# The last MLP of a two-layer trunk, its first products in pairs with seven block products in place of eight

## The chip, the cores and the metric

The kernel runs on one core of a Trainium2 chip. The metric is the device time of one execution in microseconds (us), the median of several runs. A profile of one more execution gives the times of every instruction.

## What is computed

A sequence of 528 positions (16 learned ones ahead of 512 real ones) with 1024 features goes through two layers, each a mixer followed by a squared-ReLU MLP, all float32. What the change touches is the MLP of the last layer; the learned positions are dropped at the end, so it works on 512 positions:

```python
def _sq_relu_mlp(hn, w1, w2):
    a = jax.nn.relu(hn @ w1)
    return (a * a) @ w2
...
h = h + _sq_relu_mlp(_rmsnorm(h, norm_mlp[layer]), mlp_w1[layer], mlp_w2[layer])
h = _rmsnorm(h, norm_final)
return h[:, N_META:, :]
```

Here `w1` is 1024x4096 and `w2` 4096x1024. `_rmsnorm` divides each position by the root of the mean of its squares and multiplies by a gain per feature.

## The kernel before

Activations lie feature-major: a tile has 128 features on the partitions and the positions along the free dimension. The weights come from memory as 225 units of 128x1024 (512 KB); a unit is eight 128x128 blocks, as a rule one block of 128 output features against 1024 inputs. Float32 accuracy is had from three products of a reduced format: every operand is split into a high part (a cast, ScalarE, lines 120 and 169) and a low part (the difference, VectorE, line 117), and each block costs three matmuls: high·high, high·low, low·high.

`emit_load` (line 149) brings a unit into `raw` (two buffers) and splits it into `wh` and `wl` (three buffers each). For the units in the set `POOL_L`, which holds 161 and 164 of the last MLP, GpSimd makes the low part. `get_w` keeps the loads two units ahead of use. `unit_mm` (line 206) multiplies a unit with eight pairs of activation tiles: in the last MLP 24 matmuls of 512 columns into one PSUM bank out of the four of `mmp`.

`mlp` (line 681) is used for both layers. `norm_x` (line 255) multiplies each of the eight tiles of `h` with the gain and splits it; the squares are summed on GpSimd (`nsq`, line 273). The reciprocal root (`norm_r`, line 276: four matmuls with a matrix of ones, then ScalarE and VectorE) is not applied to the input but to the output of the first product. It is asked for after the first unit. There are four quarters `q`, and each has eight first units, whose output goes through line 692 (VectorE: max with 0, times the root), line 694 (ScalarE: square), a cast (line 120) and a difference (line 117) into the activation tiles `a0` to `a7`, and then eight second units, whose output VectorE adds to `h` (line 705). The second units of the last quarter, units 217 to 224, are kept in eight buffers of their own, and `final_quarter` (line 958) uses them the other way round (positions on the partitions, lines 973 to 997), followed by the last norm and the stores. The chain of the last MLP alone is thus units 161 to 216 and then those eight.

In the first MLP (line 708) `make_ahead` (line 185) runs after every second unit: it brings the 32 units 129 to 160 into SBUF by DMAs from GpSimd's queue, splits them and writes both parts back to memory, from where the attention layer reads them without a split.

The order of instructions on each engine is made by a list scheduler at compile time: an instruction's priority is its place in the program, and `soon()` moves it ahead by 568 places. Each engine then runs its list in that order and waits at each instruction for what it needs.

Of the kernel before, what the change touches and what calls it, by code (L numbers as in the profile page):

```python
# [10 lines left out]
F32 = mybir.dt.float32  # L11
F32R = mybir.dt.float32r
# [4 lines left out]
P = 128  # L17
# [4 lines left out]
KB = 8  # L22
# [33 lines left out]
POOL_L = {5, 33, 43, 44, 52, 126, 161, 164}  # L56
N_S = 31

AHEAD = range(129, 161)

# [22 lines left out]
def trunk(tc, hT, wu, wri, pk, lv, rope, gf, out, probe=None):  # L83
# [7 lines left out]
    with ctx:  # L91
# [14 lines left out]
        def sc(name, dt=F32, w=T):  # L106

            return big.tile([P, T], dt, tag="s", name=name, bufs=N_S)

        def xt(name):  # L110
# [13 lines left out]
        pkt = cp.tile([P, N_PK], F32, name="pkt")  # L124
        nc.sync.dma_start(out=pkt, in_=pk)
        ones = cp.tile([P, P], F32, name="ones")
# [10 lines left out]
        def soon():  # L137
            return tc.high_priority(offset=BOOST)
# [11 lines left out]

        def emit_load():
            i = state["next"]
            u = seq[i]
            if i in AHEAD:
                wh, wl = (wp.tile([P, 1024], F32R, tag="w" + p, name=f"w{p}{i}") for p in "hl")
                for w, part in zip((wh, wl), parts[i - AHEAD[0]]):
                    nc.sync.dma_start(out=w.bitcast(F32), in_=part)
                ready.append((wh, wl))
                state["next"] += 1
                return  # L160
            raw = wr.tile([P, 1024], F32, tag="raw", name=f"raw{i}")
            nc.sync.dma_start(out=raw, in_=wu[u])
            if u >= N_UNIT - 8:
                wh, wl = (wp.tile([P, 1024], F32R, tag="wf" + p, name=f"w{p}{i}", bufs=8) for p in "hl")
            else:
                wh = wp.tile([P, 1024], F32R, tag="wh", name=f"wh{i}")
                wl = None if u == U_GATE else wp.tile([P, 1024], F32R, tag="wl", name=f"wl{i}")
            with soon():
# [30 lines left out]

        def get_w(u):  # L200
            while state["next"] <= min(state["use"] + 2, len(seq) - 1):
                emit_load()
            assert seq[state["use"]] == u
            state["use"] += 1
            return ready.pop(0)
# [107 lines left out]
        ident = cp.tile([P, P], F32, name="ident")  # L313
        make_identity(nc, ident)
        onesr = cp.tile([P, P], F32R, name="onesr")
# [249 lines left out]
        def conv_in(b):  # L565
            i, pr = b % 2, b // 2
            if ("gw", pr) not in lru:
                rawg = wr.tile([P, 512], F32, tag="rawg", name="rawg", bufs=1)
# [112 lines left out]
        def mlp(u0, gc, lo, tag, last=None, between=None):  # L681
            n = T - lo
            mx, terms = norm_x(h, gc, lo, tag)
            for q in range(4):
                a = []
                for j in range(KB):
                    ps = unit_mm(u0 + q * 16 + j, mx, lo, n)
                    if q == j == 0:
                        rs, _ = norm_r(terms, lo, tag)
                    t = sc("rt")  # L690
                    for p, tk in ps:
                        nc.vector.scalar_tensor_tensor(out=t[:, tk], in0=p, scalar=0.0, in1=rs[:, tk],  # L692
                                                       op0=ALU.max, op1=ALU.mult)
                    nc.scalar.activation(out=t[:, lo:], in_=t[:, lo:], func=AF.Square)  # L694
                    a.append(xt(f"a{j}"))
                    split(a[j], t[:, lo:], slice(lo, T))
                    if between and j % 2:
                        between()
                if q == 3 and last:
                    last(a)  # L700
                else:
                    for c in range(KB):
                        ps = unit_mm(u0 + q * 16 + 8 + c, a, lo, n)
                        for p, tk in ps:
                            nc.vector.tensor_tensor(out=h[:, c, tk], in0=p, in1=h[:, c, tk], op=ALU.add)  # L705
                        if between and c % 2:
                            between()

        mlp(U_MLP0, C_NMLP0, 0, "m", between=make_ahead)
# [26 lines left out]
        mkf = cp.tile([P, P], F32, name="mkf")  # L736
# [3 lines left out]
        mkr = cp.tile([P, P], F32R, name="mkr")  # L740
        nc.vector.tensor_copy(out=mkr, in_=mkf)
        idr = cp.tile([P, P], F32R, name="idr")
# [10 lines left out]
        for pair in kz:  # L753
            for c in range(2):
                nc.gpsimd.memset(pair[c][64 - 64 * c:128 - 64 * c, :].bitcast(F32), 0.0)
# [56 lines left out]
        def attn_steps(hd, rot, vr):  # L812
# [54 lines left out]
            def tstep(I):  # L867
                if I == 0:
                    st["pp"] = big.tile([P, 2, 1792], F32R, tag="y", name="pp")
# [74 lines left out]
        gfr = big.tile([P, 1024], F32, tag="gf", name="gfr")  # L944
        nc.sync.dma_start(out=gfr, in_=gf.partition_broadcast(P))
        h_t = []

        def turn_h(t):

            r = big.tile([P, 1024], F32, tag="ht", name="ht", bufs=4)  # L950
# [47 lines left out]
        mlp(U_MLP1, C_NMLP1, NM, "n", last=final_quarter)  # L998


def lay_out(x, meta_tokens, norm_mix, norm_mlp, norm_final, ab_w_in, ab_if_bias, mlstm_norm, lru_conv_w, lru_conv_b,
# [8 lines left out]
    def put(u, m):  # L1010
        wu[u, :, :, :m.shape[1]] = m.reshape(KB, P, m.shape[1]).transpose(1, 0, 2)
# [16 lines left out]
    for l, u0 in ((0, U_MLP0), (1, U_MLP1)):  # L1028
        for q in range(4):
            for j in range(8):  # L1030
                s = q * 1024 + j * P
                put(u0 + q * 16 + j, mlp_w1[l][:, s:s + P])
                if u0 + q * 16 + 8 == N_UNIT - 8:
                    wu[N_UNIT - 8 + j] = mlp_w2[l][s:s + P, :].reshape(P, KB, P)
                    continue
                put(u0 + q * 16 + 8 + j, mlp_w2[l][q * 1024:(q + 1) * 1024, j * P:(j + 1) * P])
# [57 lines left out]
```

## Time and profile before

| | us |
|---|---|
| three runs | 1461.93, 1464.75, 1466.83 (median 1464.75) |
| the profiled execution, its own time | 1463.24 |
| span of its instructions | 1461.4 |
| TensorE busy | 1437.9 |
| VectorE busy | 814.5 |
| ScalarE busy | 650.8 |
| GpSimd busy | 214.0 |

The span is what the profile sees, from the first to the last instruction; 1.84 us of the execution lie around it. The mean granted clock of TensorE is 0.999 of full speed. Busy time of TensorE counts an instruction from its start to its modelled end, so neighbouring matmuls overlap in it, and what a stage costs is better read from the distance of their starts.

### The profile page before, as it was taken

Reading aid. Unit: us, or ns where it says so; the run is one execution under the profiler, and the core shown is the slowest. Engines: PE = TensorE matmul, PEld = TensorE weight load, DVE = VectorE, ACT = ScalarE, POOL = GpSimd, SP = SyncE. Lnnn points to the kernel's source line nnn. Section 1 sums busy time; section 2 is a strip of 40 time slices with the busy share of each in tenths; the row PEclk is TensorE's granted clock in tenths of the full one; section 3 lists DMA queues with packets and bytes.
Section 4 is the critical chain, followed back from the end, with each engine's and each line's share of the span. In section 5 each row is a group of like instructions: output and inputs, shape, how many; then the busy total and the mean of one; then the engine's idle time right before and its main releaser. Section 6 shows DMA issues by size and latency. Waiting matters only on the chain. (4 is left out here: it accounts for less than half of the span.)

```text
span 1461.4 us, 24650 instructions
## 1 busy us (share of the span) xinstructions
PE 1437.9 (98%) x9970; PEld 1338.6 (92%) x9970; DVE 814.5 (56%) x1423; ACT 650.8 (45%) x1154; POOL 214.0 (15%) x286
## 2 busy tenths in 40 slices
PE   8999999999999999999999999999999999999998
PEld 8999999999999999999999998989887888888886
DVE  6867754667544545545445568777755344343452
ACT  6454743647334424334334536565644223142342
POOL 4000001010012231322314511101031000000001
PEclk9999999999999999999999999999999999999999
DMA  7332224231223685857857875555332332333331
GB/s 255 98 116 80 89 72 133 60 101 59 88 87 102 217 272 175 266 183 234 283 180 245 297 230 156 170 158 181 124 116 88 100 91 97 98 90 101 89 126 46
DMA packets 70046, 210.11 MB, mean 144 GB/s; under 512 B 13066, under 2 KB 14615, under 8 KB 69932
## 3 DMA queue, kind: packets, MB, share of 16 engines
q1 hardware_dynamic: 53996, 157.15, 34.4%
q0 software_dynamic: 15360, 50.34, 10.4%
q8 instruction: 78, 1.28, 0.4%
q10 hardware_dynamic: 576, 1.05, 0.2%
q14 instruction: 36, 0.29, 0.1%
HBM read 162.11 MB, written 35.71 MB: 135 GB/s over the span
## 5 line engine op out<-in xcount | busy, mean ns | idle before, releaser
L169 ACT CAST wh<-raw 128x1024 fp32r<-128x1024 f32 x193 | 202.6, 1050 | 503.7 <-PE mm L220 402.8
L117 DVE TENSOR_TENSOR wl<-raw,wh 128x1024 fp32r<-128x1024 f32 x184 | 227.1, 1235 | 66.9 <-ACT wh L169 66.5
L705 DVE TENSOR_TENSOR h<-mm,h 128x264 f32<-128x264 f32 (+1 forms) x88 | 41.2, 498 | 109.8 <-PE mm L220 109.8
L117 DVE TENSOR_TENSOR ral<-ra,rah 128x512 fp32r<-128x512 f32 x64 | 43.7, 688 | 56.4 <-ACT rah L120 56.4
L120 ACT CAST rah<-ra 128x512 fp32r<-128x512 f32 x64 | 39.5, 617 | 69.3 <-DMA ra<-wu 69.1
L692 DVE SCALAR_TENSOR_TENSOR rt<-mm,mrstd 128x264 f32<-128x264 f32 x64 | 24.7, 428 | 76.7 <-PE mm L220 76.7
L692 DVE SCALAR_TENSOR_TENSOR rt<-mm,nrstd 128x512 f32<-128x512 f32 x32 | 22.1, 692 | 79.2 <-PE mm L220 79.1
L273 POOL TENSOR_TENSOR nsq<-nsq 128x528 f32<-128x528 f32 (+1 forms) x28 | 46.2, 1652 | 93.1 <-ACT nsq L271 87.8
L982 POOL TENSOR_TENSOR zg<-z,gfr 128x512 f32<-128x512 f32 x4 | 5.2, 1296 | 342.0 <-DVE z L980 336.2
L785 POOL TENSOR_TENSOR qr<-qr,tb 128x512 f32<-128x512 f32 (+1 forms) x16 | 24.6, 1536 | 166.5 <-DVE qs L784 159.1
L117 POOL TENSOR_TENSOR wl<-raw,wh 128x1024 fp32r<-128x1024 f32 x8 | 19.2, 2403 | 201.6 <-ACT wh L169 120.4
L853 ACT ACTIVATE e<-psc,mx 128x264 f32<-128x264 f32 (+3 forms) x80 | 38.2, 482 | 9.1 <-DVE mx L846 8.1
L846 DVE TENSOR_REDUCE mx<-psc 128x1 f32<-128x264 f32 (+3 forms) x80 | 33.2, 430 | 15.5 <-PE psc L844 7.8
L694 ACT ACTIVATE rt<-rt 128x528 f32<-128x528 f32 (+1 forms) x64 | 40.6, 636 | 2.8 <-DVE rt L692 2.8
L197 POOL DMA_DIRECT2D ra<-wu x64 | 34.7, 547 | 2.9 <-issue 2.9
L663 DVE TENSOR_TENSOR h<-mm,h 128x264 f32<-128x264 f32 x32 | 12.2, 426 | 38.0 <-PE mm L220 38.0
L120 ACT CAST rh<-qr 128x512 fp32r<-128x512 f32 (+1 forms) x16 | 10.0, 627 | 51.2 <-DVE qr L787 48.2
L365 POOL TENSOR_SCALAR_AFFINE_SELECT cb<-cb 128x128 f32<-128x128 f32 (+2 forms) x20 | 7.7, 397 | 166.3 <-DMA cb<-crow 166.1
L886 ACT CAST pp<-pt 128x128 fp32r<-128x128 f32 (+2 forms) x64 | 21.0, 342 | 16.4 <-PE pt L874 14.4
L220 PE MATMUL mm<-ax0h,wh 128*128 128x264 f32 x98 | 22.0, 297 | 6.3 <-ACT ax0h L262 6.3
L840 PE MATMUL psc<-st,st 128*128 128x264 f32 (+3 forms) x80 | 26.4, 331 | 1.3 <-ACT e L853 0.9
L117 DVE TENSOR_TENSOR pp<-pt,pp 128x128 fp32r<-128x128 f32 (+2 forms) x64 | 23.8, 382 | 3.6 <-ACT pp L886 3.5
(866 smaller groups left out, 4908.7 us busy)
## 6 DMA issues: line engine op xcount, KB each, us to landing
raw<-wu SPq DMA_DIRECT2D x193, 512.0 KB
ra<-wu POOLq DMA_DIRECT2D x64, 256.0 KB, 5.0
h<-hT SPq DMA_DIRECT2D x16, 264.0 KB
st<-rh SPq DMA_DIRECT2D x32, 132.0 KB
kz<-rl SPq DMA_DIRECT2D x16, 132.0 KB
st<-rh SPq DMA_DIRECT2D x16, 128.0 KB
st<-rl SPq DMA_DIRECT2D x16, 128.0 KB
cb<-crow SPq DMA_DIRECT2D x4, 264.0 KB
```

The lines of the kernel that those rows point to most:

```text
L117: eng.tensor_tensor(out=o, in0=a, in1=b, op=ALU.subtract)
L120: nc.scalar.copy(hl[0][:, sl], src)
L169: nc.scalar.copy(wh, raw)
L197: nc.gpsimd.dma_start(out=raw, in_=wu[seq[i]][:, c])
L273: nc.gpsimd.tensor_tensor(out=fin[0][:, lo:], in0=fin[0][:, lo:], in1=sq[:, lo:], op=ALU.add)
L692: nc.vector.scalar_tensor_tensor(out=t[:, tk], in0=p, scalar=0.0, in1=rs[:, tk], op0=ALU.max, op1=ALU.mult)
L694: nc.scalar.activation(out=t[:, lo:], in_=t[:, lo:], func=AF.Square)
L705: nc.vector.tensor_tensor(out=h[:, c, tk], in0=p, in1=h[:, c, tk], op=ALU.add)
L785: pool_or_dve("mM"[w]).tensor_tensor(out=raw[:, lo:], in0=raw[:, lo:], in1=tb[0][:, lo:], op=ALU.mult)
L840: nc.tensor.matmul(d[:, :m], qS[c][:, qs], kS[c][:, s0:s0 + m], start=True, stop=False)
L846: nc.vector.tensor_reduce(out=mx[:, 2 * c + r:2 * c + r + 1], in_=d[:, :m], axis=AX.X, op=ALU.max, negate=True)
L853: nc.scalar.activation(out=e[:, s0:s0 + m], in_=d[:, :m], func=AF.Exp, bias=mx[:, 2 * c:2 * c + 1], accum_out=ss[:, c + 2 * r:c + 2 * r + 1])
```

## The change

The last MLP gets code of its own in place of the call of `mlp`. Units 161 to 224 hold the same weights in another order. `ORDER1` lists it: five single first units; then three times a second unit and a first unit; a second unit; then eight times a pair of first units and two second units; then four times a pair and one second unit; then the last eight units as before. That is 8 single first units, 12 pairs and 24 second units.

A pair is a product of a 2x2 block matrix of weights (two blocks of 128 outputs, two halves of the 1024 inputs: the even and the odd tiles) with a 2x2 block matrix of activations (the same halves of the inputs, two halves of 256 positions). Done directly it takes eight block products, each of 4 x 3 matmuls of 256 columns (or, as before, 48 matmuls of 512 columns for the two units). `pair_mm` does seven (g1, g6, g5, g2, g7, g3, g4), that is 84 matmuls of 256 columns, in three PSUM banks X, Y, Z, of which each is added to after a part of it has been read out: X by ScalarE after g1, Y and Z by VectorE (`plus`) after g6, g5 and g7. It needs sums of the weight blocks (`sums`, `rest`) and sums of the activation blocks (`pair_x`, once, for all pairs). The root is applied in `pair_x`, so the pairs' outputs only go through relu, square and split.

A second unit now holds two blocks of outputs against four activation tiles (512 of the 4096 inputs): 2 x 12 matmuls of 512 columns in two banks, and two additions to `h`. `second` runs its halves; the seventh product of the pair before stands between the first two halves that follow it.

`feed`, after each step, brings one more load or one part of a pair's weight preparation, up to four units ahead. `norm_r` comes after the second unit.

```diff
-POOL_L = {5, 33, 43, 44, 52, 126, 161, 164}
+POOL_L = {5,33,43,44,52,126}
+N_W = 4
+N_XB = 2
+XS_FROM = 1
+SCRATCH = 8192
+LOOK = 4
+ORDER1 = [("o", i) for i in range(5)]
+for _j in range(3):
+    ORDER1 += [("w", 0, _j), ("o", 5 + _j)]
+ORDER1.append(("w", 0, 3))
+for _e in range(1, 5):
+    for _j in range(2):
+        ORDER1 += [("p", 2 * _e + 2 + _j), ("w", _e, 2 * _j), ("w", _e, 2 * _j + 1)]
+for _j in range(4):
+    ORDER1 += [("p", 12 + _j), ("w", 5, _j)]
...
+        def split_w(name, raw, n=1024, bufs=N_W):
+            hl = [wide(wp, n, F32R, tag=f"v{p}" if n == 1024 else f"wd{p}", name=name + p, bufs=bufs) for p in "hl"]
+            nc.scalar.copy(hl[0], raw)
+            sub(nc.vector, hl[1], raw, hl[0].bitcast(F32))
+            return hl
+        def emit_pair():
+            i = state["next"]
+            raw = wide(wr, 2048, F32, tag="rawp", name=f"rawp{i}", bufs=1).rearrange("p (a c) -> p a c", a=4)
+            load(raw.rearrange("p (u a) c -> p u (a c)", u=2), wu[i:i + 2].rearrange("u p c -> p u c"))
...
+            def first():
+                with soon():
+                    it["A"] = split_w(f"A{i}_", raw[:, 0:2, :])
+            def sums():
+                s4 = it["s4"] = wide(wr, 2048, F32, tag="sums", name=f"sums{i}", bufs=1).rearrange(
+                    "p (a c) -> p a c", a=4)
+                with soon():
+                    nc.vector.tensor_tensor(out=s4[:, 0:4:2], in0=raw[:, 0:4:3],
+                                            in1=raw[:, 2:3].to_broadcast([P, 2, 512]), op=ALU.add)
+                    nc.vector.tensor_tensor(out=s4[:, 3], in0=s4[:, 2], in1=raw[:, 0], op=ALU.add)
+                    it["S"] = split_w(f"S{i}_", s4[:, 2:4])
+            def last():
+                with soon():
+                    it["D"] = split_w(f"D{i}_", raw[:, 3], 512, 1)
+            def rest():
+                s4 = it["s4"]
+                with soon():
+                    nc.vector.tensor_tensor(out=s4[:, 1], in0=s4[:, 3], in1=raw[:, 1], op=ALU.add)
+                    it["U"] = split_w(f"U{i}_", s4[:, 0:2])
...
+        def pair_mm(i, xs, n, done):
...
+            def product(b, w, c, x, ks=range(4), more=False):
...
+                wh, wl = it[w]
+                for k in ks:
+                    cc = slice(c * 512 + k * P, c * 512 + (k + 1) * P)
+                    h_, l_ = (v[:, x, :hv] for v in xs[k])
+                    for j, (ww, xx) in enumerate(((wh, h_), (wh, l_), (wl, h_))):
+                        nc.tensor.matmul(st[b][:, :hv], ww[:, cc], xx, start=st[b, "n"] == 0,
+                                         stop=k == 3 and j == 2, skip_group_check=True)
...
+            def g1(ks=range(4)):
...
+                ps = product("X", "A", 0, B11, ks)
+                if 3 in ks:
+                    with soon():
+                        state["p1"] = nc.scalar.copy(st["h"][0], ps)
+            def g6(ks=range(4)):
+                ps = product("Y", "S", 1, N2, ks)
+                if 3 in ks:
+                    plus(st["h"][1], ps, st["h"][0])
+            def g5(ks=range(4)):
+                ps = product("Z", "S", 0, N1, ks)
+                if 3 in ks:
+                    plus(st["h"][2], ps, st["h"][0])
+            def g2():
+                ps = product("X", "A", 1, B21)
+                with soon():
+                    relu(st["t"][0][:, s1], ps)
+            def g7():
+                plus(st["t"][2][:, s2], product("Y", "U", 0, T3), st["h"][2])
+            def g3():
+                plus(st["h"][3], product("Z", "U", 1, B22), st["h"][1])
+                relu(st["t"][0][:, s2], st["h"][3])
+                done(st["t"][0])
+            def g4():
+                t, c2 = st["t"][1:]
+                plus(c2[:, s1], product("Y", "D", 0, T4), st["h"][0])
+                relu(t[:, lo:], c2[:, lo:], -1.0)
+                done(t)
+            return g1, g6, g5, g2, g7, g3, g4
...
+        def pair_x(h, gc, lo, rs, k):
+            hv = (T - lo) // 2
+            b = big.tile([P, 8, HV], F32, tag="xb", name="xb", bufs=N_XB)[:, :, :hv]
+            xp = big.tile([P, 14, HV], F32R, tag="xp", name=f"xp{k}", bufs=4)
+            hi, low = xp[:, 0:7], xp[:, 7:14]
+            for i, o in ((0, slice(0, 8, 7)), (1, slice(1, 3))):
+                nc.vector.scalar_tensor_tensor(out=b[:, o, :], in0=h[:, k + i, lo:].rearrange("p (a c) -> p a c", a=2),
+                                               scalar=pc(gc + k + i),
+                                               in1=rs[:, lo:].rearrange("p (a c) -> p a c", a=2),
+                                               op0=ALU.mult, op1=ALU.mult)
+            b11, b21, b22, n1, t3, n2, t4, b12 = (b[:, i, :] for i in range(8))
+            sub(nc.vector, b[:, 3:5, :], b[:, 0:3:2, :], b[:, 7:8, :].to_broadcast([P, 2, hv]))
+            nc.vector.scalar_tensor_tensor(out=n2, in0=t3, scalar=-1.0, in1=b11, op0=ALU.mult, op1=ALU.subtract)
+            nc.vector.scalar_tensor_tensor(out=t4, in0=n2, scalar=-1.0, in1=b21, op0=ALU.mult, op1=ALU.subtract)
+            nc.scalar.copy(hi[:, :, :hv], b[:, 0:7, :])
+            sub(nc.vector, low[:, :, :hv], b[:, 0:7, :], hi[:, :, :hv].bitcast(F32))
+            return hi, low
...
-        mlp(U_MLP1, C_NMLP1, NM, "n", last=final_quarter)
+        x1, terms = norm_x(h, C_NMLP1, NM, "n")
+        xs, rs1, act, came1 = [], [], [], []
...
+        steps1, held = [], []
+        for place, t in zip(PLACE1, ORDER1):
+            if t[0] == "p":
+                steps1 += [(place, g) for g in held]
+                p = pair_mm(place, xs, NR, done)
+                steps1 += [(place, g) for g in p[:-1]]
+                held = [p[-1]]
+            else:
+                w = second(place, *t[1:]) if t[0] == "w" else [functools.partial(first, place)]
+                steps1 += [(place, w[0])] + [(place, g) for g in held + w[1:]]
+                held = []
+        k = 0
+        for n, (place, g) in enumerate(steps1):
+            g()
+            if n >= XS_FROM and k < KB:
+                xs.append(pair_x(h, C_NMLP1, NM, rs1[0], k))
+                k += 2
+            feed(min(place + LOOK, N_UNIT - 8))
+        load(gfr, gf.partition_broadcast(P))
+        final_quarter(act[24:])
```

Beside that: the last gain (`gfr`) is loaded after the steps and no longer at the start; the casts of units 217 to 224 come behind ScalarE's copy after the last pair's g1; the loads of the last MLP are kept in order on SyncE's queue; the units of the last MLP have split buffers of their own, four of each; several tiles are rounded up to multiples of 264 columns or put together into one tile; half as much of SBUF is set aside for the descriptors of GpSimd's DMAs (`SCRATCH`); and in the first MLP `make_ahead` runs three times more, after unit 4 of the first three quarters.

## Rows read from the trace of the kernel before

**Rows 1.** The page, parts 1 and 2 (40 equal slices of the span).

```profile
PE 1437.9 (98%) x9970; PEld 1338.6 (92%) x9970; DVE 814.5 (56%) x1423; ACT 650.8 (45%) x1154; POOL 214.0 (15%) x286
...
PEclk9999999999999999999999999999999999999999
```

**Rows 2.** The chain that ended last, its end: start us, us, what.

```profile
1100.87 0.86 PE nps L282 x4
1101.73 305.20 PE mm L220 x1320
...
1407.81 11.10 PE mf L973 x48
...
1443.71 11.15 PE mf L973 x72
```

**Rows 3.** Length, busy PE, PEld, DVE, ACT, POOL, clock, DMA share, GB/s.

```profile
1101.73:1406.94 305.21, 305.21 (x1323) 247.79 (x1322) 128.94 (x145) 98.62 (x125) 2.42 (x1) 1.00 0.32 98
```

**Rows 4.** Timeline of TensorE, the last 48 matmuls: start us, us.

```profile
1449.08 0.28 PE L973 MATMUL mf<-wh,a0h 128*128 128x256 f32 x1
...
1454.57 0.28 PE L973 MATMUL mf<-wl,a7h 128*128 128x256 f32 x1
```

**Rows 5.** Timeline of the weight loads beside those matmuls, first and last.

```profile
1449.32 0.19 PEld L973 LDWEIGHTS mf<-wh,a1h 128*128 128x128 f32 x1
...
1454.45 0.19 PEld L973 LDWEIGHTS mf<-wl,a7h 128*128 128x128 f32 x1
```

**Rows 6.** Groups by line, 1100 to 1462 us: count, busy us, mean ns.

```profile
L117 DVE TENSOR_TENSOR wl<-raw,wh 128x1024 fp32r<-128x1024 f32 x60 | 73.4, 1226 | 15.6 <-ACT wh L169 15.6
L169 ACT CAST wh<-raw 128x1024 fp32r<-128x1024 f32 x61 | 64.1, 1052 | 214.1 <-PE mm L220 198.4 <-DMA raw<-wu 10.3 <-issue 5.3
L692 DVE SCALAR_TENSOR_TENSOR rt<-mm,nrstd 128x512 f32<-128x512 f32 x32 | 22.1, 692 | 79.2 <-PE mm L220 79.1
L694 ACT ACTIVATE rt<-rt 128x512 f32<-128x512 f32 x32 | 20.1, 630 | 0.0
```

**Rows 7.** Groups by line and shape, 400 to 1462 us, VectorE and ScalarE.

```profile
L705 DVE TENSOR_TENSOR h<-mm,h 128x264 f32<-128x264 f32 x64 | 24.6, 425 | 28.2 <-PE mm L220 28.2
L778 ACT ACTIVATE qr<-mm 128x264 f32<-128x264 f32 x16 | 5.3, 382 | 0.0
```

**Rows 8.** One instruction of tile nx0l: ns min/median/max, start.

```profile
L263 DVE SCALAR_TENSOR_TENSOR nx0l<-h,pkt,nx0h x1: 744/744/744, 1084.2 to 1084.2; 128x512 fp32r<-128x512 f32 x1
```

**Rows 9.** Two stretches of the attention layer, columns as in group 3.

```profile
890.00:915.00 25.00, 23.85 (x159) 20.83 (x158) 19.76 (x50) 15.08 (x45) 2.28 (x2) 1.00 0.52 156
965.00:990.00 25.00, 24.79 (x173) 22.59 (x172) 18.55 (x50) 14.58 (x44) 3.12 (x2) 1.00 0.58 180
```

**Rows 10.** TensorE's waits, whole span: us in total, times, longest.

```profile
PE mm L220 <- DVE nx6l L263: 2.1, 1, 2.1
PE mm L220 <- DVE nx7l L263: 0.7, 1, 0.7
```

**Rows 11.** Timeline of VectorE at the entry of the last MLP.

```profile
1094.40 2.33 DVE L117 TENSOR_TENSOR wl<-raw,wh 128x1024 fp32r<-128x1024 f32 x1
1096.66 1.74 DVE L263 SCALAR_TENSOR_TENSOR nx6l<-h,pkt,nx6h 128x512 fp32r<-128x512 f32 x1
1098.32 1.76 DVE L263 SCALAR_TENSOR_TENSOR nx7l<-h,pkt,nx7h 128x512 fp32r<-128x512 f32 x1
...
1105.87 0.69 DVE L253 SCALAR_TENSOR_TENSOR nrstd<-rqa,rqy 128x512 f32<-128x512 f32 x1
```

**Rows 12.** Timeline of ScalarE, casts of the last units' weights.

```profile
1408.34 1.05 ACT L169 CAST wh<-raw 128x1024 fp32r<-128x1024 f32 x1 [2.26 <-DMA raw<-wu]
...
1414.18 1.05 ACT L169 CAST wh<-raw 128x1024 fp32r<-128x1024 f32 x1 [1.77 <-DMA raw<-wu]
```

**Rows 13.** Busy us, end of the first MLP; page part 6, DMA issues.

```profile
822.00:830.00 8.00, 8.00 (x54) 7.32 (x53) 5.16 (x8) 4.01 (x8) 7.67 (x7) 1.00 0.98 373
ra<-wu POOLq DMA_DIRECT2D x64, 256.0 KB, 5.0
```

More of the change, by code (lines that the diff above doesn't have):

```diff
@@ L678, in trunk @@
         dump("h1", h)
[L681 to L707, printed above, removed]
@@ L709, in trunk @@
-        mlp(U_MLP0, C_NMLP0, 0, "m", between=make_ahead)
+        mx, terms = norm_x(h, C_NMLP0, 0, "m")
+        for q in range(4):
+            a = []
+            for j in range(KB):
+                ps = unit_mm(U_MLP0 + q * 16 + j, mx)
+                if q == j == 0:
+                    rs, _ = norm_r(terms, 0, "m")
+                t = sc("rt")
+                for p, tk in ps:
+                    nc.vector.scalar_tensor_tensor(out=t[:, tk], in0=p, scalar=0.0, in1=rs[:, tk],
+                                                   op0=ALU.max, op1=ALU.mult)
+                nc.scalar.activation(out=t, in_=t, func=AF.Square)
+                a.append(xt(f"a{j}"))
+                split(a[j], t)
+                if j % 2 or j == 4 and q < 3:
+                    make_ahead()
+            for c in range(KB):
+                ps = unit_mm(U_MLP0 + q * 16 + 8 + c, a)
+                for p, tk in ps:
+                    nc.vector.tensor_tensor(out=h[:, c, tk], in0=p, in1=h[:, c, tk], op=ALU.add)
+                if c % 2:
+                    make_ahead()
@@ L754, in trunk @@
             for c in range(2):
[L755 removed]
+                in_turn("kz", lambda: nc.gpsimd.memset(pair[c][64 - 64 * c:128 - 64 * c, :].bitcast(F32), 0.0))
         steps = []
@@ L997, in final_quarter, with done, first @@
                     nc.sync.dma_start(out=out[t * P:(t + 1) * P, 512:1024], in_=z2)
-        mlp(U_MLP1, C_NMLP1, NM, "n", last=final_quarter)
+        x1, terms = norm_x(h, C_NMLP1, NM, "n")
+        xs, rs1, act, came1 = [], [], [], []
+        def done(t):
+            nc.scalar.activation(out=t[:, NM:], in_=t[:, NM:], func=AF.Square)
+            act.append(xt("a"))
+            split(act[-1], t[:, NM:], slice(NM, T))
+        def first(i):
+            w = get_w(i)
+            ps = mmt("mn")
+            for k in range(KB):
+                b = slice(k * P, (k + 1) * P)
+                for n, (ww, xx) in enumerate(((0, 0), (0, 1), (1, 0))):
+                    nc.tensor.matmul(ps, w[ww][:, b], x1[k][xx][:, NM:], start=k == n == 0, stop=k == KB - 1 and n == 2)
+            came1.append(ps)
+            if i == U_MLP1:
+                return
+            if not rs1:
+                rs1.append(norm_r(terms, NM, "n")[0])
+            while came1:
+                t = sc("rt")
+                with soon():
+                    nc.vector.scalar_tensor_tensor(out=t[:, NM:], in0=came1.pop(0), scalar=0.0, in1=rs1[0][:, NM:],
+                                                   op0=ALU.max, op1=ALU.mult)
+                done(t)
@@ new lines, in second, with half @@
+        def second(i, e, j):
+            def half(c):
+                if "w" not in w:
+                    w["w"] = get_w(i)
+                ps = mmt("mw")
+                for k in range(4):
+                    b = slice((4 * c + k) * P, (4 * c + k + 1) * P)
+                    for n, (ww, xx) in enumerate(((0, 0), (0, 1), (1, 0))):
+                        nc.tensor.matmul(ps, w["w"][ww][:, b], act[4 * e + k][xx][:, NM:], start=k == n == 0,
+                                         stop=k == 3 and n == 2)
+                f = 2 * j + c
+                with soon():
+                    nc.vector.tensor_tensor(out=h[:, f, NM:], in0=ps, in1=h[:, f, NM:], op=ALU.add)
+            w = {}
+            return [functools.partial(half, c) for c in range(2)]
```

123 lines of the change are left out of this document (92 added, 31 removed).

## The prediction, made before the changed kernel was run

> **What bounds the kernel now.** I began with the page: TensorE is busy 98% of the span, VectorE 56%, ScalarE 45%, and the clock row is full throughout [rows 1]. Busy time of overlapping matmuls says little, so I went to the chain of waits: from 1101.73 us to the end of unit 216 it is one piece of TensorE, 305.20 us for 55 units of 24 matmuls, and the final units follow with hardly a break [rows 2]. That is 305.20 / 1320 = 231.2 ns for a matmul of 512 columns, and a unit costs 5.55 us. Over the same stretch VectorE is busy 128.94 and ScalarE 98.62 of 305.21 us [rows 3]. So in this stage time is matmul columns, and the change takes columns away and pays with VectorE work.
>
> **What a pair costs TensorE.** Before, two first units are 48 matmuls x 231.2 ns = 11.10 us. After, 84 matmuls of 256 columns. The trace has 48 of those at its very end: their starts run from 1449.08 to 1454.57 us, 47 steps, 116.8 ns each [rows 4], and their weight loads keep the same step although each lasts 0.19 us [rows 5]. The whole last piece agrees: 24 x 231.2 + 48 x 116.8 = 11.15 us [rows 2]. A pair is 84 x 116.8 = 9.81 us, 1.29 us less; 12 pairs give **15.5 us**. Second units keep 24 matmuls of 512 columns.
>
> The row thus says that half the columns take half the time. The Trainium skill's page "TensorE: Matmul & The Clock Gate", section "Back-to-back issue gap", says otherwise: pairs of load and matmul sustain about 131 ns at 512 columns and 81 ns at 128, so that short matmuls pay much more per column. On a line through its two figures a 256-column matmul would take 98 / 131 of a long one, and by that a pair, as an estimate, 14.5 us in place of 11.1: a loss of 41 us. Both step times measured here contradict it.
>
> **What a pair costs VectorE.** Prices: 1.226 us for 1024 elements, 0.692 for 512 [rows 6], 0.425 for an eviction of 264 columns, which I take for 256 [rows 7]. Splits of A, S, U, D: 3 x 1.226 + 0.692 = 4.37. Weight sums: one of 1024 and two of 512, 2.61. Five evictions (`plus`): 2.13. Low parts of the two outputs: 1.38. Together 10.5 us, where two first units cost 2 x (1.226 + 0.692 + 0.692) = 5.2. A second unit costs 1.226 + 2 x 0.692 = 2.61 in place of 1.92. So a pair with two second units gives VectorE 15.7 us of work beside 9.81 + 11.10 = 20.9 us of TensorE (75%), and a pair with one, 13.1 beside 15.4 (85%). ScalarE has, for a pair, casts of 3 x 1.052 + 0.63, a copy and two relus of 256 columns at 0.382 [rows 7], a relu, two squares and two casts at 0.63 [rows 6]: 8.1 us, and 1.05 more per second unit, under 60%. TensorE stays the bound if nothing queues. On the path each pair hands over three banks: X goes back to TensorE after g6 and g5, Y after g5 and g2, Z after g2 and g7, each with two products, 2.8 us, as cover; an eviction is 0.4 us behind at most one running instruction of 1.2 us.
>
> How much TensorE idles beside so busy a VectorE the attention layer bounds: 24.79 busy of 25 us with VectorE at 74% (0.8% idle), 23.85 of 25 at 79% (4.6%) [rows 9]. Those chains are tighter, with no cover counted in microseconds; below, nothing. The pair stretch lasts 8 x 20.9 + 4 x 15.4 = 229 us: 0 to 10.5 us. I take 0.8% for the first 167 us and, VectorE being fuller, 2% for the last 62: **+2.5 us**.
>
> **The entry.** TensorE lost 2.8 us in unit 161 to the low parts of the last two normed tiles [rows 10], which stood on VectorE behind a weight split and were slow, 1.74 and 1.76 us, beside GpSimd's sum of squares [rows 11]; alone such an instruction takes 0.744 [rows 8]. That chain stays. The splits of units 161 and 164 move to VectorE: the first falls into gaps, but with four buffers in place of three, unit 164's can now come ahead of those two tiles: 1.2 to 2.3 us. The norm's four matmuls move behind unit 162, and a wait of 0.4 us for the sum goes. Between -0.4 and +3.5; I take **+1.3**.
>
> **The opening.** The root comes 5.55 us later, so not at 1106.56 [rows 11] but about 1113.4. `pair_x` costs VectorE 2 x 0.744 + 0.692 + 2 x 0.425 + a difference of 1792 elements, 1.75 x 1.226 = 2.15: 5.2 us, four times. The first second unit needs activation 3 about 1127.3 (1101.73 + 1.3 + four units + nine matmuls). In those 13.9 us VectorE has four evictions and four low parts (5.5), two weight splits (2.5) and two `pair_x` (10.4), which precede activation 3 in the program: 18.4 us. TensorE waits 4.5 us if VectorE keeps that order, nothing if the scheduler moves `pair_x` back while it waits for ScalarE's cast (1.84 us each). I take **+1.5**, nearer to nothing since the rest of `pair_x` is not due before the first pair, over 35 us later.
>
> **The end.** The eight final units come in through two buffers; casts at 1408.34 and, two units on, at 1414.18 [rows 12] make 2.9 us per unit, and the last split ends some 1 us before the seventh activation's turn (1407.81 + 7/8 x 11.10 = 1417.5). After, their casts wait for the last pair's first product, 15.4 us ahead of the final stage; `gfr` is now a 512 KB load among them, up to 2.9 us; and the last addition to `h` ends only as its transposes begin, 1.0 us. Between -0.5 and +4; I take **+1.0**.
>
> **Elsewhere.** `make_ahead` finishes three calls earlier, which relieves the DMA engines where they are full, at 98% with TensorE shown busy all the same [rows 13]; half the room for descriptors can make GpSimd's queue wait a landing, 5.0 us [rows 13], beside the 11 us or more that two units give most calls. Other buffers' places may cost or give a microsecond. I take 0, between -1 and +1.
>
> **Sum.** -15.5 + 2.5 + 1.3 + 1.5 + 1.0 = -9.2 us. The profiled execution took 1463.24 us (span 1461.4 and 1.84 around it); it becomes 1454.0. The median of the runs, 1464.75, stands 1.5 above it, so the forecast is **1455.5 us**.
>
> **The rivals.**
> 1. *Thin cover.* The whole pair stretch idles 4.6%, 10.5 us in place of 2.5, and the opening keeps its order (4.5): 1455.5 + 8 + 3 = 1466; with the first alone 1463.5. For it: VectorE goes from 42% to 75 and 85%. Against: evictions are emitted ahead of the next pair's weights. Chance 0.15, time 1463.5.
> 2. *Evictions behind weights: slower.* If the scheduler lets a pair's sums (1.226 + 0.692), the split of S (1.226) and U's sum and split (0.692 + 1.226) stand ahead of one eviction (0.425), a bank comes back after 5.5 us, not 2.8: 2.7 us lost per pair, 32 in all in place of 2.5, 1485 us. It decides from 0.97 us per pair, (9.2 + 2.5) / 12, on. For it: all of these carry the same head start, and each engine keeps its order. Against: U's sum comes four steps after the sums, and its buffer only becomes free late. Chance 0.14.
> 3. *Loads bound.* If loads of 0.19 us no longer overlapped each other, a pair would cost 84 x 0.188 = 15.8 us, 56 more in all and no gain: 1527. The step of the loads speaks against it [rows 5]. The Trainium skill's rule above is its nearest kin. Chance 0.02.
>
> That pairs do not shorten TensorE's work at all I leave out: the matmuls are written out one by one.
>
> **How the numbers follow.** The forecast has 0.69 and, by its terms, 1448 to 1460; no stall anywhere would be 1448.3 (1464.75 - 15.5 - 0.4 - 0.5). Adding rival 1 takes the range to 1467; rivals 2 and 3 and a little at the low end are left out. A measurement can tell 0.3%, 4.4 us: faster is below 1460.4, slower above 1469.1. Faster 0.68, the same 0.16, slower 0.16.
>
> **What would show it.** TensorE should have 432 matmuls more, in steps of 117 ns inside pairs; a pair and two second units should take about 20.9 us; VectorE should be busy near 75 and then 85% there. Waits of TensorE for `plus`, for U's or S's low part or for ScalarE's copy of X of over 1 us in each pair would show rival 2; waits at the first second unit behind `pair_x` the upper bound of the opening; waits for the final units' low parts that of the end. A step above 120 ns would make the main term wrong.

## The result, and the profile after

The changed kernel takes 1455.45 us, the median of four runs (1453.67 to 1456.42), against 1465.6 for the kernel before in the runs beside it: a ratio of 0.9933, 95% interval 0.9912 to 0.9955. The forecast was 1455.5. The profiled execution took 1453.67 us (span 1451.9), 9.6 less than the one before, where the sum had said 9.2. So the total is right; the sections below show that its parts are not all right.

The page of the changed kernel, its part 1 and one line of part 6 (DMA issues: the weights of the 12 pairs):

```profile
PE 1428.6 (98%) x10402; PEld 1354.0 (93%) x10402; DVE 901.9 (62%) x1569; ACT 695.2 (48%) x1230; POOL 207.0 (14%) x284
...
rawp<-wu SPq DMA_DIRECT2D x12, 1024.0 KB
```

Against [rows 1] TensorE has 432 matmuls more and is still busy 98% of a shorter span: 9.3 us less of it. VectorE paid 87 us.

The chain that ended last, in the last MLP of the changed kernel (start us, us, what):

```profile
1111.28 16.68 PE mn L1192 x72
...
1179.57 8.34 PE mw L1214 x36
1200.61 8.34 PE mw L1214 x36
...
1433.85 11.21 PE mf L1151 x72
```

It is still TensorE's work. Two neighbouring groups of second products start 1200.61 - 1179.57 = 21.04 us apart: one pair and two second units. Take away two units of 5.55 and a pair costs 9.94 us, 84 x 118.3 ns, not 9.81.

Stretches of the changed kernel: entry and opening, the units before the pairs, all pairs, and the pairs that have one second unit each (columns as in [rows 3]):

```profile
1095.80:1127.90 32.10, 29.83 (x126) 23.03 (x125) 25.19 (x31) 19.08 (x27) 7.64 (x5) 1.00 0.34 103
1127.90:1166.80 38.90, 38.90 (x170) 31.53 (x169) 36.63 (x46) 16.73 (x19) 0.00 (x0) 1.00 0.22 78
1166.80:1397.10 230.30, 230.30 (x1491) 209.36 (x1490) 163.96 (x222) 114.25 (x164) 0.00 (x0) 1.00 0.33 107
1333.96:1397.06 63.10, 63.10 (x439) 58.70 (x438) 45.47 (x64) 35.45 (x52) 0.00 (x0) 1.00 0.36 121
```

In the pairs TensorE is busy in all of 230.30 us, with VectorE at 71% (163.96 / 230.30), and at 72% in the last four pairs. No wait of TensorE stands in that stretch. All the idle time of the last MLP is in the first row, the entry:

```profile
PE mn L1192 <- DVE nx3l L435: 0.7, 1, 0.7
PE mn L1192 <- DVE nx5l L435: 0.7, 1, 0.7
PE mn L1192 <- DVE nx2l L435: 0.5, 1, 0.5
PE mn L1192 <- DVE nx4l L435: 0.3, 1, 0.3
```

These are TensorE's waits (us in total, times, longest), where [rows 10] had two, of 2.1 and 0.7 us.

**Where the time went, by marks on TensorE.** From the first matmul on nx0h to the last of the final products: 362.8 us before (1091.8 to 1454.57 [rows 4]), 348.9 after (1095.82 to 1444.76), so the last MLP alone gained 13.9. But the changed kernel reaches it 4.0 us later. From mx0h to dx0h, the first MLP, it needs 375.2 us in place of 372.7; up to mx0h 1.6 us more; between dx0h and nx0h 264.8 both times. In total -13.9 + 2.5 + 1.6 = -9.8; behind the last matmul the changed kernel takes 0.2 us more. The 2.5 us in a stage whose matmuls the change leaves alone were not foreseen.

### The profile page after: what moved, and what is told of

It reads as the page before. It is cut to its first block, busy times and chain, and to the rows that moved or that the text cites. A ratio compares the mean times of both kernels' runs of the same rounds, so it can differ in the third digit from the quotient of the medians.

```text
span 1451.9 us, 25701 instructions
## 1 busy us (share of the span) xinstructions
PE 1428.6 (98%) x10402; PEld 1354.0 (93%) x10402; DVE 901.9 (62%) x1569; ACT 695.2 (48%) x1230; POOL 207.0 (14%) x284
## 3 DMA queue, kind: packets, MB, share of 16 engines
q10 hardware_dynamic: 576, 1.05, 0.2%
## 4 chain that ended last, share of the span: by engine, by line
PE 88%; ACT 3%; issue 3%; DVE 3%; POOL 1%; DMA 1%; SPq 0%; POOLq 0%; DVEq 0%; ACTq 0%
PE mm L392 55%; PE mw L1214 9%; PE mpY L311 4%; PE mf L1151 3%; PE mn L1192 3%; PE mpZ L311 2%; PE mpX L311 2%; PE mo L1115 2%; PE pnum L612 1%; PE po L1077 1%; PE pss L594 1%; PE pg L805 1%; PE pt L1053 1%; POOL nsq L464 1%; PE psc L1019 0%
## 5 line engine op out<-in xcount | busy, mean ns | idle before, releaser
L208 ACT CAST wh<-raw 128x1024 fp32r<-128x1024 f32 x169 | 175.5, 1046 | 143.8 <-PE mw L1214 41.5
L142 DVE TENSOR_TENSOR wl<-raw,wh 128x1024 fp32r<-128x1024 f32 x162 | 199.6, 1233 | 28.9 <-ACT wh L208 27.3
L1214 PE MATMUL mw<-ah,wh 128*128 128x512 f32 x192 | 75.6, 394 | 0.0
L1214 PE MATMUL mw<-al,wh 128*128 128x512 f32 x192 | 75.5, 393 | 0.0
L1214 PE MATMUL mw<-ah,wl 128*128 128x512 f32 x192 | 75.5, 393 | 0.0
L889 DVE TENSOR_TENSOR h<-mm,h 128x264 f32<-128x264 f32 x64 | 24.6, 426 | 46.5 <-PE mm L392 46.5
L1214 PEld LDWEIGHTS mw<-ah,wl 128*128 128x128 f32 x192 | 36.1, 188 | 8.4
L1214 PEld LDWEIGHTS mw<-al,wh 128*128 128x128 f32 x192 | 36.1, 188 | 7.3
L1214 PEld LDWEIGHTS mw<-ah,wh 128*128 128x128 f32 x192 | 36.0, 188 | 7.3
L1025 DVE TENSOR_REDUCE mx<-psc 128x1 f32<-128x264 f32 (+3 forms) x80 | 33.1, 429 | 14.1 <-PE psc L1023 7.0
L852 DVE TENSOR_TENSOR h<-mm,h 128x264 f32<-128x264 f32 x32 | 12.3, 427 | 41.7 <-PE mm L392 41.7
L1218 DVE TENSOR_TENSOR h<-mw,h 128x512 f32<-128x512 f32 x48 | 32.9, 686 | 7.3 <-PE mw L1214 7.2
```

The source lines that it names most:

```text
L142: eng.tensor_tensor(out=o, in0=a, in1=b, op=ALU.subtract)
L1025: nc.vector.tensor_reduce(out=mx[:, 2 * c + r:2 * c + r + 1], in_=d[:, :m], axis=AX.X, op=ALU.max, negate=True)
L1214: nc.tensor.matmul(ps, w["w"][ww][:, b], act[4 * e + k][xx][:, NM:], start=k == n == 0, stop=k == 3 and n == 2)
```

## The experiments

**The two kernels once more.**

> The kernel before, unchanged, profiled once more. The profile of the changed kernel reached the attention layer 4.1 us later than that of the kernel before, because matmuls of 264 columns came every 121.2 ns in the first MLP in place of 120.4. If that is the difference between two executions, this profile has another step too, between 120.2 and 121.4 ns, and it reaches the attention layer anywhere between 826 and 831 us. If it belongs to the edits outside the last MLP (places of buffers, descriptor room, three more calls of make_ahead), this profile repeats 120.4 +- 0.1 ns and 827 us.

Measured: 1465.07 us; mx0h to dx0h 372.73 us, the 264-column step (from the start of one matmul of 264 columns to the next) as before, the last MLP 362.8.

> The changed kernel, unchanged, profiled once more. If the slower step of short matmuls belongs to the kernel, it repeats: 121.2 +- 0.1 ns in the first MLP, 118.5 ns inside the pairs, attention reached at 831 us. If it belongs to the execution, it moves by half a per cent or more. Ratio to the kernel before either way 0.991 to 0.996.

Measured: 1455.4 us, ratio 0.9943 (0.9928 to 0.9958); mx0h to dx0h 375.30. The later arrival is therefore the kernel's and no chance, except for the start: mx0h comes at 454.2 and 456.0 in two traces of the kernel before, at 455.8 and 457.3 in two of the changed one. All the runs below taken together, it comes at 454.2 to 456.6 in the five traces of the kernel before and its variants (mean 455.3) and at 455.8 to 458.1 in the nine of the changed kernel and its variants (mean 457.3). Windows of the same 290 us of the first MLP, first before, then changed:

```profile
480.00:770.00 290.00, 290.00 (x2402) 290.00 (x2401) 146.83 (x227) 110.92 (x153) 80.74 (x150) 1.00 0.70 227
```

```profile
480.00:770.00 290.00, 290.00 (x2385) 290.00 (x2384) 147.65 (x232) 112.55 (x158) 89.96 (x167) 1.00 0.72 241
```

TensorE is busy without a gap and at full clock in both, yet has 17 matmuls fewer in one. In the timelines, the starts give a step of 120.9 ns before and 121.7 after.

**The main term: eight products in place of seven.** A first product computed twice makes 96 matmuls of 256 columns per pair.

```diff
             def g1(ks=range(4)):
                 if "it" not in st:
                     start()
+                ps = product("X", "A", 0, B11, ks)
+                st["X", "n"] = 0
                 ps = product("X", "A", 0, B11, ks)
                 if 3 in ks:
```

> Each pair computes its first product twice (the second time over the first, so the result is the same): eight products in place of seven, nothing else changed. If TensorE's matmuls are the path in the pair stretch, it costs 12 x 12 x 118.5 ns = 17.1 us and the kernel is about 1472, slower than the kernel before by 7 (ratio to it about 1.005). If VectorE is the path there (rival 2), TensorE's extra 1.4 us per pair is hidden in waits and the cost is below 5 us.

Measured: 1473.06 us, ratio 1.0061 (1.0044 to 1.0078), 17.7 above the changed kernel beside it; TensorE waits nowhere in the pairs. 144 further matmuls cost what the step says (144 x 118.3 ns = 17.0 us), and with eight products the change would be a loss. So the gain of the last MLP comes from the product that is left out.

**How much room VectorE has.** Every low part of a weight is made twice in the pairs:

```diff
-            sub(nc.vector, hl[1], raw, hl[0].bitcast(F32))
+            for _ in range(2):
+                sub(nc.vector, hl[1], raw, hl[0].bitcast(F32))
```

> Each of a pair's four weight splits makes its low part twice: 3 x 1.22 + 0.68 = 4.35 us more of VectorE per pair, 52 us in all. VectorE was busy 71% in the pair stretch; this makes it 92% of the eight first periods (20.9 us) and about 100% of the four last (15.4 us). If VectorE had room to spare, as the absence of any wait of TensorE suggests, the cost is 0 to 5 us, all of it in the last four periods. If evictions queue behind weight work as soon as VectorE is fuller, TensorE waits in every period, over 1 us each, 12 us or more in all.

Measured: 1456.52 us, ratio 0.9949 (0.9934 to 0.9964), 1.1 above the changed kernel. The window of its pairs:

```profile
1166.80:1397.10 230.30, 230.30 (x1492) 209.47 (x1491) 208.54 (x270) 112.86 (x162) 0.00 (x0) 1.00 0.30 99
```

VectorE is busy 208.54 of 230.30 us, 91%, and TensorE has still no gap: from the first pair to the final stage it needs 230.98 us, against 230.95 in the changed kernel. A busy share alone does not tell of stalls, then. What may count instead is how long each result may take; the next run takes that time away.

**The cover.** The products of a pair follow each other so that each bank is wanted again at once or after one product:

```diff
-            return g1, g6, g5, g2, g7, g3, g4
+            return g1, g2, g6, g5, g7, g3, g4
...
-                        nc.tensor.matmul(st[b][:, :hv], ww[:, cc], xx, start=st[b, "n"] == 0,
-                                         stop=k == 3 and j == 2, skip_group_check=True)
+                        in_turn("pe", lambda: nc.tensor.matmul(
+                            st[b][:, :hv], ww[:, cc], xx, start=st[b, "n"] == 0,
+                            stop=k == 3 and j == 2, skip_group_check=True))
```

The matmuls of the second units are put in turn in the same way, so that the order on TensorE is fixed by hand. Fixing it does nothing by itself: in the trace of the changed kernel the products and second units of all 12 pairs already stand in the order of the program. What changes is the place of g2.

> Edit: inside a pair the products follow one another as g1, g2, g6, g5, g7, g3, g4 and TensorE's order is fixed by hand, so that the PSUM bank of a block is wanted again at once (X: by g2 straight behind g1) or after one product (Y, Z) and no four-block product lies between. Nothing of the work is left out. If the place of the second products is what covers the sums and the evictions, X alone costs a cast of 0.7 us or more per pair and the whole pair 0.7 to 1.2 us, so 8 to 14 us over 12 pairs: 1463 to 1470, and the waits of TensorE name ScalarE's cast of the first product and VectorE's sums. If the pairs have so much room that the order doesn't matter: 1455 to 1457.

Measured: 1469.48 us, ratio 1.0037 (1.0024 to 1.005): 14.1 above the 1455.4 of the changed kernel. TensorE's waits in its pairs, and two windows of its entry:

```profile
PE mpX L311 <- ACT hh L341: 4.6, 11, 0.5
PE mpY L311 <- DVE hh L319: 0.8, 2, 0.5
```

```profile
1104.00:1106.00 2.00, 1.12 (x2) 0.40 (x2) 0.35 (x1) 0.49 (x1) 1.48 (x1) 0.63 0.00 0
1106.00:1108.00 2.00, 1.19 (x3) 0.83 (x3) 1.21 (x2) 2.00 (x5) 1.27 (x1) 0.50 0.00 0
```

From the first pair to the final stage it needs 240.9 us in place of 230.95: 0.83 per pair. X is wanted at once, and its copy on ScalarE shows as the wait of 0.4 to 0.5 us; TensorE's idle time in the pairs is 5.4 us, the loss 10. The rest is presumably the way to ScalarE and back, while TensorE still shows as busy; that is argued, not shown. So the cover is what makes the pairs worth doing: of the 13.9 us that the last MLP gained, 10 are lost without it. Another 3.2 us lie in the entry: there the schedule came out another way, TensorE idled for longer, and after that the granted clock was 0.50 (1.2 of 2.4 GHz) for some microseconds, as the second window shows. That part says nothing of the cover.

**The entry.** First, the squares' sum moved behind the low parts, on the same engine:

```diff
-        x1, terms = norm_x(h, C_NMLP1, NM, "n")
+        x1, last1 = norm_x(h, C_NMLP1, NM, "n", late=True)
+        terms = []
+        with tc.issue_after(last1.ins):
+            for i in range(KB):
+                norm_sq(h, NM, i, terms)
```

> Edit: at the entry of the last MLP the squares and their sum on GpSimd come after the low parts of the normed blocks, not beside them. Nothing is left out. If VectorE's low parts take 1.77 us (nx3l to nx5l of the changed kernel) instead of 0.74 (nx6l, nx7l) because GpSimd adds squares at the same time, they fall to about 0.75 each, TensorE's 3.5 us of idle time in the first two units falls to 0.5 to 1.5, and the time falls by 2 to 3 us, to 1452.4 to 1453.4, if the sum of squares still arrives before the first activation needs it. If it arrives late, the first activation (nrstd, 1115 us) comes some 5 us later and the first second products wait for it: 1455 to 1459. If GpSimd has no part in it: 1.77 us again and 1455.4.

Measured: 1458.49 us, ratio 0.9961 (0.9947 to 0.9975), 3 above the changed kernel. Its timeline of VectorE, then of GpSimd, then TensorE's longest wait:

```profile
1100.85 0.75 DVE L435 SCALAR_TENSOR_TENSOR nx5l<-h,keep,nx5h 128x512 fp32r<-128x512 f32 x1
1101.52 1.80 DVE L435 SCALAR_TENSOR_TENSOR nx6l<-h,keep,nx6h 128x512 fp32r<-128x512 f32 x1
...
1104.93 2.30 DVE L142 TENSOR_TENSOR wl<-raw,wh 128x1024 fp32r<-128x1024 f32 x1
```

```profile
1101.30 12.02 POOL L464 TENSOR_TENSOR nsq<-nsq 128x512 f32<-128x512 f32 x7 [72.08 <-ACT nsq L462]
```

```profile
PE nps L473 <- POOL nsq L464: 2.9, 1, 2.9
```

The sums now begin at 1101.30, and from that moment a low part takes 1.80 us instead of 0.75. The changed kernel shows it the other way round: nx3l to nx5l take 1.77, 1.78 and 1.76 us beside GpSimd's sums, nx6l and nx7l, after them, 0.74. So GpSimd's sums are what slows the low parts, but the time is lost again at the norm, since seven sums take 12.02 us in this place. The Trainium skill's page "SBUF — State Buffer", section "Who interferes with whom", has the rule: a VectorE instruction with two inputs in SBUF and a GpSimd instruction that reads SBUF exclude each other for a whole instruction. These rows agree: the low part grows by about 1.05 us, and the weight split beside the same sums, which takes 1.22 us alone, by 1.08, not by a share of its own length.

So GpSimd should have only what it can do before VectorE is in a hurry, and VectorE the rest, which it does faster (0.69 us where GpSimd takes 1.3 alone):

```diff
-                if not late:
+                if not late and k < vec:
                     norm_sq(h, lo, k, fin)
+            for k in range(vec, KB):
+                norm_sq(h, lo, k, fin, nc.vector, low)
...
-        x1, terms = norm_x(h, C_NMLP1, NM, "n")
+        x1, terms = norm_x(h, C_NMLP1, NM, "n", vec=3)
```

(`low` is the last low part, behind which these sums are issued.)

> Edit: of the seven sums of squares at the entry of the last MLP the first two stay on GpSimd, early, and the last five go to VectorE behind its eight low parts. Nothing is left out. If the 1.77 us of nx3l to nx5l come from GpSimd's sums beside them, as the run with the late squares showed in turn (0.75 us without, 1.80 with), the low parts take 0.75 us each, five sums add 5 x 0.69 = 3.4 us to VectorE behind them, where it was idle for 5.95 us, the sum of squares is there before TensorE asks for it, and TensorE's 2.2 us of waits for low parts go to 1.0 or less without a wait at the norm: 1453.0 to 1454.4. If the sum comes late all the same, TensorE waits at the norm: 1455 to 1458.

Measured: 1452.49 us (1451.9 to 1452.69), ratio 0.9918 (0.9904 to 0.9931).

> The changed kernel once more, on the same chip as the runs beside it: 1455.4 us, the 264-column step at 121.7 ns and the way from mx0h to dx0h at 375.2 us.

Measured beside it: 1454.99 us, ratio 0.9931 (0.9917 to 0.9945); 375.19 us and 121.7 ns. VectorE at the entry of the version with the sums moved:

```profile
1103.17 0.75 DVE L435 SCALAR_TENSOR_TENSOR nx7l<-h,keep,nx7h 128x512 fp32r<-128x512 f32 x1
1103.84 2.14 DVE L467 TENSOR_TENSOR nsq<-nsq 128x512 f32<-128x512 f32 x3
1105.89 1.22 DVE L142 TENSOR_TENSOR wl<-raw,wh 128x1024 fp32r<-128x1024 f32 x1
1107.03 1.41 DVE L467 TENSOR_TENSOR nsq<-nsq 128x512 f32<-128x512 f32 x2
```

The low parts from nx2l on take 0.75 us, and TensorE has no wait left in the entry: from nx0h to the first second product 28.6 us in place of 32.0. That is 3.4 us in the trace and 2.5 between the medians. This version beats both kernels; it came out 0.5 us below the expected range, which had left TensorE up to 1.0 us of waits.

**The slower step: two suspects alone.** Both are edits of the kernel before: the smaller scratch, and with it weight tiles rounded up to 1056 columns.

```diff
-    nc = bacc.Bacc("TRN2", target_bir_lowering=False, num_devices=1)
+    nc = bacc.Bacc("TRN2", target_bir_lowering=False, num_devices=1, dynamic_dma_scratch_size=8192)
```

> The kernel before with one edit: the scratch for DMA descriptors in SBUF is 8192 bytes, as in the changed kernel, not the default 16384. Read: the step of the 264-column matmuls (120.9 ns in both traces of the kernel before, 121.7 ns in all four of the changed kernel and its variants so far) and the way from mx0h to dx0h (372.7 against 375.2 us). If the scratch is the cause of the slower step: 121.7 ns and 375.2. If it is the places of the weight tiles, or the program itself: 120.9 ns and 372.7.

Measured: 121.1 ns, 373.24 us, 1463.87 us in all.

> The kernel before with two edits: the scratch of 8192 bytes, and the weight tiles and their raw tiles rounded up to 1056 columns as in the changed kernel, so that weights lie at many places of SBUF instead of at two remainders of 4096. Read as in the run with the scratch alone. If the places are the cause: 121.7 ns and 375.2 us. If the program itself (the three further calls of make_ahead, the order of instructions) is: 120.9 ns and 372.7.

Measured: 121.2 ns, 373.57 us, 1465.14 us. Neither forecast is met: each edit makes the first MLP a little slower, together by 0.84 of the 2.46 us that lie between the two kernels there.

**The step: the further calls of make_ahead.**

```diff
-                if j % 2 or j == 4 and q < 3:
+                if j % 2:
                     make_ahead()
```

> Edit: the changed kernel without its three further calls of make_ahead in the first MLP, so that its weights for the attention are prepared at the same places as in the kernel before. Nothing is left out. If those calls make the 264-column step slower there: 120.9 to 121.2 ns, 372.7 to 373.6 us from mx0h to dx0h, and 1453.0 to 1454.2. If the places of the tiles in SBUF are the cause, which the scratch and the rounded weight tiles explained in part (121.07 and 121.22 ns against 120.86 and 121.74): 121.7 ns, 375.2 us and 1455.4.

Measured: 121.7 ns and 375.21 us, so the calls are not the cause; and 1461.42 us (1460.23 to 1463.23), ratio 0.998 (0.9971 to 0.9989): 6.4 above the changed kernel, where a gain or nothing was expected. TensorE's waits around dx0h, and the window of that place:

```profile
PE mm L392 <- DVE dx7l L435: 1.2, 1, 1.2
PE mm L392 <- ACT dx7h L434: 0.7, 1, 0.7
PE nps L473 <- POOL nsq L464: 0.4, 1, 0.4
```

```profile
840.00:850.00 10.00, 8.57 (x50) 7.86 (x51) 4.01 (x7) 4.77 (x7) 2.10 (x3) 0.83 0.74 261
```

GpSimd's queue does the last preparations until 831 us, and only then the seven sums of squares for the attention's norm, in one run of 10.75 us beside VectorE's low parts of the same norm: the collision of the entry once more, at another place (dx5l to dx7l take 1.87, 1.62 and 1.63 us, with the calls 0.77 each). TensorE idles 2.3 us, and after that the granted clock is 0.83 in the mean of these 10 us, with 0.50 from 844 to 846 (1.00 throughout with the calls). From dx0h to nx0h it takes 269.9 us in place of 266.0 in the run beside it and 264.8 to 265.0 in the two other traces of the changed kernel; the rest of the 6.4 us between the medians is not placed (the two profiled executions stand 4.4 apart). With the three calls the last preparation is over by 805 us and the sums come one by one as their blocks are ready. The kernel before has the collision too (10.80 us of sums from 822.57, dx5l to dx7l of 1.89, 1.61 and 1.68 us), but 2.6 us earlier against dx0h, and TensorE waits only 0.4 us there. So the calls are a gain only against the changed kernel without them; why that version is later with its sums than the kernel before stays open.

**The step: places.** The scratch alone had moved 471 of the kernel's 912 tiles down by exactly 8192 bytes. An idle tile of that size, alive from the first instruction to the last, puts 888 of them back.

```diff
+        space = cp.tile([P, 2048], F32, name="space")
+        nc.vector.memset(space[:, 0:1], 0.0)
         pkt = cp.tile([P, N_PK], F32, name="pkt")
...
+                    nc.vector.tensor_tensor(out=space[:, 1:2], in0=y, in1=space[:, 0:1], op=ALU.mult)
```

> The kernel before with the scratch of 8192 bytes and an idle tile of 8192 bytes that puts 888 of the 912 tiles in SBUF back at the places that they have in the kernel before (the run with the scratch alone had most of them 8192 bytes lower). Nothing is left out. Read as there: 120.86 ns a step and 372.7 us from mx0h to dx0h were those of the kernel before, 121.07 ns and 373.25 us those with the scratch alone. If the places of the tiles set the step: 120.9 ns and 372.7 us. If the smaller scratch does: 121.07 ns and 373.2 us.

Measured: 1463.95 us, 120.9 ns and 372.73 us, those of the kernel before. The window in this kernel:

```profile
480.00:770.00 290.00, 290.00 (x2401) 290.00 (x2401) 147.14 (x227) 110.92 (x153) 80.41 (x150) 1.00 0.70 227
```

So in this pair of runs the places of the tiles set the step, not the size of the scratch. The 256-column step moves with them, and by more: the last 48 matmuls with the smaller scratch alone, then with the tiles put back:

```profile
1449.77 0.28 PE L973 MATMUL mf<-wh,a0h 128*128 128x256 f32 x1
...
1455.31 0.28 PE L973 MATMUL mf<-wl,a7h 128*128 128x256 f32 x1
```

```profile
1449.77 0.28 PE L975 MATMUL mf<-wh,a0h 128*128 128x256 f32 x1
...
1455.25 0.28 PE L975 MATMUL mf<-wl,a7h 128*128 128x256 f32 x1
```

That is 117.9 ns and 116.6 (5.54 and 5.48 us over 47 steps, so good to some 0.2 ns), against 116.8 in [rows 4]. That the whole slower step of the changed kernel comes from its places is the natural reading, and only argued: in the first MLP the order of the matmuls and the clock are the same and the calls are excluded, but no run gave its tiles the old places, which its larger buffers do not allow.

## Why the prediction was right, and where its steps were not

- **Main term, -15.5: mis-sized by 1.6.** Confirmed as a mechanism by the eighth product (+17.7). The step taken from [rows 4], 116.8 ns, is 118.1 in the same 48 matmuls of the changed kernel (1439.21 to 1444.76), and 118.3 inside pairs: 1008 matmuls x 1.5 ns = 1.5 us. I took a step for a property of the shape; it also belongs to the kernel's layout, as the 117.9 ns of the kernel before with its tiles moved show.

```profile
1439.21 0.28 PE L1151 MATMUL mf<-wh,ah 128*128 128x256 f32 x1
...
1444.76 0.28 PE L1151 MATMUL mf<-wl,ah 128*128 128x256 f32 x1
```

- **Stalls in the pairs, +2.5: wrong reason.** It was 0. Reading idle shares from the attention [rows 9] at a like busy share of VectorE was the failed step, as VectorE at 91% without a stall shows. The prediction's other argument, two products of cover against an eviction of 0.4 us, was the right one, and the tight order confirms it. VectorE's share was also overestimated (71% and 72% for 75% and 85%). The prices held, an addition of 256 columns taking 0.42 us; but neighbouring VectorE instructions overlap a little in the trace, as nx5l and nx6l above, where the second starts 0.67 us after the first, which lasts 0.75.
- **Entry, +1.3: 0.** The weight splits did come ahead of the low parts as feared, and the low parts were slow for the reason given; but TensorE had the matmuls of unit 162 to take in between, so the time lost stayed the same: 9.97 us before from nx0h to the end of unit 161 and the norm (1091.76 to 1101.73) where 24 steps and the norm need 6.4, 3.6 lost, and 32.0 now where the version without waits needs 28.6, 3.4 lost. The reason was worth more than the term: removing the collision gains 2.5 us.
- **Opening, +1.5: 0.** The chain runs from the first products into the second ones at 1127.80 without a break. Activation 3's low part starts at 1126.78 and takes 0.69 us, and TensorE needs it in the eleventh matmul of that second unit, at 1130.1: 2.6 us in time, since the scheduler put parts of `pair_x` between the activations and not ahead of them.
- **End, +1.0: 0.1.** From the first final matmul to the last 47.1 us (1397.65 to 1444.76) against 47.0. The weights came in time. Making low parts twice brought a wait of 0.3 us there, so the reserve is not large.
- **Elsewhere, 0 between -1 and +1: wrong, about +4.** "Other buffers' places may cost or give a microsecond" was the right term and mis-sized: 2.5 us in the first MLP alone, and up to mx0h 1.6 in the profiled executions, of which a part may be the scatter of the start (1.8 us between two traces of one kernel). The smaller room for descriptors shows no cost in GpSimd's transfers, which land after 4.9 us in place of 5.0. And I gave the earlier end of `make_ahead` no worth. Against the kernel before it shows none (264.8 us from dx0h to nx0h in both), but without it the changed kernel would be 6.4 us slower.

The sum came out right because 6.2 us of foreseen stalls that did not happen stand against 5.7 (1.6 + 2.5 + 1.6) of slower steps and a later start that were not foreseen. That the two cancel is luck. Rival 1 (thin cover) and rival 2 (evictions behind weights) named the true danger: the tight order shows that 0.83 us per pair is lost as soon as the cover goes. In the change as made neither occurs. Rival 3 is refuted by the step of 118 ns.

## What to carry to other kernels

When work is traded from TensorE to VectorE, count the time between a result and its next use, not VectorE's busy share: here 91% cost no gap in the pairs, and taking the products from between the two uses of a bank (both of X's, one each of Y's and Z's) cost 0.8 us per pair. Look for GpSimd instructions beside VectorE instructions with two inputs in SBUF at every place where TensorE waits for one result, such as a norm's entry, and give GpSimd only what is over before. A change that adds buffers moves all the others; measure a stage whose work it does not touch before crediting or blaming the one that it does.

## What was not expected of the hardware

Matmuls of 264 and 256 columns step faster or slower with the places of the tiles, at full clock and with TensorE never idle: 120.9 against 121.1 ns and 116.6 against 117.9 in two versions of the kernel before that differ in little else. The changed kernel has 121.7 and 118.1, and there the places are the likely cause, not a shown one. Matmuls of 512 columns changed less (231.2 ns in [rows 2]; 16.68 us for 72, or 231.7, in the chain above). Which property of the places does it stays open. And a short idle time of TensorE can cost more than itself: after 2.3 us of waits at dx0h, in the version without the three calls, the granted clock was 0.83 in the mean of a stretch of 10 us, after 3.3 us of waits at the last entry of the tight order it was 0.50 (1.2 GHz) in a stretch of 2, while the changed kernel's own entry, with 2.2 us of waits in four pieces, kept 1.00.
